# Expert loop of a two-layer block on one core: halves made by one engine less, rows gathered one expert earlier, and a branch hint on TensorE

## The chip, the cores and the metric

The kernel runs on one NeuronCore of a Trainium2 chip. The core has five engines that run side by side, each with an instruction stream of its own: TensorE (PE, matrix products; its weight loads are listed apart as PEld), VectorE (DVE), ScalarE (ACT), GpSimd (POOL) and SyncE (SP), which here issues DMAs. The metric is the device time of one execution in microseconds. It was 3232.24 us as the median of 3 runs (3224.29 to 3240.48).

## The reference

The reference is two transformer blocks on 512 tokens of width 1024, all in fp32. The first block has a hybrid mixer and then a mixture of experts, the second two attention layers with MLPs. The change touches the mixture of experts of the first block alone:

```python
def moe_ffn(h, router_w, router_bias, w_gate, w_up, w_down, ...):
    ...
    _, e_idx = lax.top_k(jnp.where(expert_mask, biased, -jnp.inf), TOP_K)      # 8 of 64 experts a token
    gate = jnp.take_along_axis(scores, e_idx, axis=1)
    gate = gate / jnp.sum(gate, axis=-1, keepdims=True) * ROUTED_SCALE
    ...
    def expert_block(args):                       # 128 rows of one expert
        xb, e = args
        return (jax.nn.silu(xb @ w_gate[e]) * (xb @ w_up[e])) @ w_down[e]
    ...
    routed = jax.ops.segment_sum(yb * row_gate[:, None], row_tok, num_segments=T + 1)[:T]
```

Each token goes to 8 of 64 experts, so an expert has 64 rows on average. The weights of an expert are 1024 x 512 (gate and up) and 256 x 1024 (down), 3 MB in fp32.

## The kernel before

A product in fp32 is made as three products: each operand is split into a high half (`hi`, rounded by ScalarE, L191) and the rest (`lo`, the difference, L192, by VectorE or POOL), and `mm3` (L220 to L222) multiplies hi by hi, hi by lo and lo by hi.

The weights of an expert come as three tiles of 1 MB (128 x 2048): two of gate and up, one of down. They land in a ring of 8 buffers (`raw`). SyncE issues them in order, in `fetch`; ahead of each it reads a word of the tile two issues back (L1144), so that no more than about two are under way. Each tile is split in two steps of 1024 columns, `halve` and `halve_to`. Of the down tile, the first step's `lo` is VectorE's and the second's POOL's; every other `lo` is VectorE's.

The rows of an expert are gathered from a table in memory by an indirect DMA of POOL (`gather`, L1213), up to 128 rows in a first block, and the results are added to an output table by another (`scatter`, L1218). The tile `cnt` holds the number of rows of each expert. `fewest` picks by comparisons on POOL a gather or scatter of 16, 32, ... 128 rows. `xg` is a list of four row buffers: two for the first blocks (`e % 2`), two for the others.

The loop over the experts is written out in Python, 64 experts and two more turns, under a manual schedule, so that every engine runs its part in the order of the code. In turn `e`:

- SyncE issues the down tile of expert `e + 1` and the gate and up tiles of `e + 2`;
- TensorE makes gate and up of expert `e` (24 products into `bank_g`), and all engines load the count of `e`;
- POOL gathers the first rows of expert `e + 2`; the halves of the down tile of `e` are made; the results of `e - 2` are copied out by ScalarE and scattered; the halves of the gate and up tiles of `e + 1` follow;
- then a branch of every engine on `n > 128` (L1377). The Then arm has a second block of 128 rows and, nested, a third and a fourth (`more_blocks`); the Else arm holds what most experts need: the transposes of the next expert's rows (`xT.turn`, L1255), the down product of `e - 1` (12 products), and the transposes of the activation (L1283).

On TensorE the Then arm, with its nested blocks, stands between the branch and the Else arm.

Of the kernel before, what the change touches and what calls it, by code (L numbers as in the profile page):

```python
# [10 lines left out]
F32 = mybir.dt.float32  # L11
# [9 lines left out]
D = 1024  # L21
NE = 64
T = 512
# [115 lines left out]
def body(tc, ins, out, stop=None, dump=None):  # L139
    nc = tc.nc  # L140
    top = ExitStack()
    V, S, G, PE = nc.vector, nc.scalar, nc.gpsimd, nc.tensor
# [10 lines left out]
    with top:  # L153
# [985 lines left out]
        def fetch(e, a):  # L1139

            if e < NE:
                ahead.append((e, a))
                if len(ahead) > 2 and ahead[-3] in raws:
                    nc.sync.value_load(raws[ahead[-3]][0:1, 0:1].bitcast(I32))  # L1144
                r = raws[e, a] = mp.tile([128, 2048], F32, tag="raw", bufs=8, name="raw")
                dma(r, ins["w_dn"][e] if a == 2 else ins["w_gu"][e, a])

        tt = mp.tile([128, 4, NE, 2], F32, name="tt")
        xg = xt
        with ExitStack() as st:  # L1150
            p = pool(st, "route")
            for e in range(2):
# [29 lines left out]
        with ExitStack() as st:  # L1182
# [54 lines left out]
                choose(0, 128)  # L1237

            def first_rows(e):
                fewest(e, gather, xg[e % 2])  # L1240

            def more_rows(e):
                with tc.If(rows(e) > 128):
                    gather(e, 1, xg[2 + e % 2])

            class Rows:

# [75 lines left out]
            st.enter_context(tc.manual_schedule())  # L1323
            for a in range(2):
                halve(0, a)
            for e in range(2):
                first_rows(e)
                more_rows(e)
            xT = Rows(xg[0], [psum("tr", 2) for _ in range(2)])
            xT.turn()  # L1330
            xT.halves()
# [4 lines left out]
            for t in (*pair, bank_t, bank_y):  # L1336
                V.memset(t, 0.0)
            y = None
            for e in range(NE + 2):
                if e == NE - 1:  # L1340

                    spare = [mp.tile([128, 2048], F32, tag="raw", bufs=8, name="raw") for _ in range(6)]
                    for j, src in enumerate((mod("m1", 5), ins["ln2_g"], ins["ln2_b"])):
                        load_row(spare[j // 2][:, j % 2 * D:(j % 2 + 1) * D], src)
                    for i in range(NT):
                        dma(spare[4 + i // 2][:, i % 2 * D:(i % 2 + 1) * D],
                            x1d[i * 128:(i + 1) * 128, :])
                if e < NE:
                    fetch(e + 1, 2)
                    fetch(e + 2, 0)  # L1350
                    fetch(e + 2, 1)
                    gate_up(gu[e], xT, bank_g)
                    n = nc.values_load(cnt[0:1, e:e + 1], min_val=0, max_val=T,
                                       engines=[E.PE, E.Activation, E.DVE, E.Pool])
                if e + 2 < NE:
                    first_rows(e + 2)
                if 0 < e <= NE:
                    act_halves(bank_t)
                if e < NE:
                    halve(e, 2, (V, G))  # L1360
                if e > 1:
                    y = rows_out(n=2)
                    down_out(pair, y)
# [5 lines left out]
                last = e == NE - 1  # L1369
                if not last:  # L1370
                    halve(e + 1, 0)
                    xT = Rows(xg[(e + 1) % 2], [psum("tr", 2) for _ in range(2)])
                    gu1 = [hl_tiles()]
                a = act(bank_g, e, 0)
                yx = rows_out("x")
                x = Rows(xg[2 + e % 2], (bank_x, bank_y))
                with tc.If(n > 128) as c:  # L1377

                    x.turn()
                    with tc.If(rows(e) > 256):  # L1380
# [17 lines left out]
                    with tc.If(n > 256):  # L1398
                        more_blocks(e, x, yx)
                        if not last:  # L1400

                            xT.halves()
                with c.Else():
                    if not last:
                        xT.turn()
                        xT.halves()
                    if e:
                        down(dn[e - 1], pair)
                    act_t(a, bank_t)
                    if not last:  # L1410
                        halve_to(gu1, e + 1, 1, 0)
# [527 lines left out]
```

## Time and profile before

| | us |
|---|---|
| median of 3 runs | 3232.24 |
| the profiled execution | 3234.01 |
| its span, first to last instruction | 3232.2 |
| expert stage, read as the window 960 to 1830 us | 870 |
| TensorE busy in that window | 744.23 |
| VectorE / ScalarE / POOL busy in that window | 642.38 / 573.62 / 390.15 |

The profiled execution is one run of the program; its span is 1.8 us shorter than its time. A busy time is the sum of the stretches in which an engine had an instruction at work. Idle time is given with its releaser, that is, with what the profile shows to have ended the wait.

### The profile page before, as it was taken

The numbers are of one execution on the slowest core, as the hardware profiler recorded it, in microseconds if no ns is written. First come the engines' busy times: TensorE is split into PE (matmuls) and PEld (weight loads), VectorE is DVE, ScalarE is ACT, GpSimd is POOL, SyncE is SP. The second block draws the span as 40 slices with busy tenths as digits, with TensorE's granted clock in tenths as the row PEclk, the third lists the DMA queues.
The fourth block names the chain that finished last, engine by engine and source line by source line (L and its number), as shares of the span: only waits on it lengthen the run. The fifth ranks groups of instructions, "written<-read, shape, count | busy, mean of one in ns | idle before, by whom it ended". The sixth has DMA issues, their size and how long they took to land. (4 is left out here: it accounts for less than half of the span.)

```text
span 3232.2 us, 42331 instructions
## 1 busy us (share of the span) xinstructions
PE 2914.3 (90%) x14268; PEld 2379.7 (74%) x14268; DVE 2118.9 (66%) x3558; ACT 1544.8 (48%) x2588; POOL 1115.8 (35%) x887
## 2 busy tenths in 40 slices
PE   7999999999778888988888579998999999889998
PEld 5887887877666766776667366676877788678887
DVE  8887876554748887885666469667554643774446
ACT  4443342555227676675665354545443434752222
POOL 3212211678334444453444321435453200320002
PEclk8999999999879999999999789998999999999999
DMA  6223314765348989897878522315443243332222
GB/s 238 74 73 118 135 68 161 243 236 204 138 155 290 315 266 299 272 322 243 288 243 273 154 89 78 110 52 199 172 161 136 72 144 111 106 109 88 91 91 72
DMA packets 142979, 540.44 MB, mean 167 GB/s; under 512 B 23809, under 2 KB 37121, under 8 KB 118017
## 3 DMA queue, kind: packets, MB, share of 16 engines
q1 hardware_dynamic: 106832, 422.21, 36.9%
q0 software_dynamic: 35760, 113.48, 12.5%
q8 instruction: 193, 3.16, 0.4%
q14 instruction: 194, 1.58, 0.2%
HBM read 509.43 MB, written 36.35 MB: 169 GB/s over the span
## 5 line engine op out<-in xcount | busy, mean ns | idle before, releaser
L192 DVE TENSOR_TENSOR lo<-raw,hi 128x1024 fp32r<-128x1024 f32 x615 | 873.8, 1439 | 453.0 <-ACT hi L191 447.0
L191 ACT CAST hi<-raw 128x1024 fp32r<-128x1024 f32 x697 | 716.3, 1053 | 477.9 <-PE mm L222 198.8
L221 PE MATMUL mm<-hlo,hi 128*128 128x512 f32 (+1 forms) x1448 | 539.2, 373 | 15.7 <-DVE hlo L962 15.7
L220 PE MATMUL mm<-hhi,hi 128*128 128x512 f32 (+1 forms) x1448 | 541.7, 376 | 5.1 <-ACT hhi L961 5.1
L222 PE MATMUL mm<-hhi,lo 128*128 128x512 f32 (+1 forms) x1448 | 538.1, 372 | 3.9 <-DVE lo L192 3.9
L221 PEld LDWEIGHTS mm<-hlo,hi 128*128 128x128 f32 x1448 | 281.7, 195 | 61.9 <-DVE hlo L962 16.8
L220 PEld LDWEIGHTS mm<-hhi,hi 128*128 128x128 f32 x1448 | 280.4, 194 | 55.4 <-ACT hhi L961 6.1
L222 PEld LDWEIGHTS mm<-hhi,lo 128*128 128x128 f32 x1448 | 281.3, 194 | 50.4 <-DVE lo L192 5.7
L355 POOL TENSOR_TENSOR ada_acc<-ada_acc,ada_w 128x512 f32<-128x512 f32 x168 | 248.5, 1480 | 138.7 <-ACT ada_acc L353 101.2
L192 POOL TENSOR_TENSOR lo<-raw,hi 128x1024 fp32r<-128x1024 f32 x82 | 208.1, 2542 | 153.2 <-ACT hi L191 82.9
L220 PE MATMUL mm<-hi,xh 128*128 128x512 f32 x584 | 235.3, 403 | 13.8 <-ACT xh L1262 5.5
L222 PE MATMUL mm<-hi,xl 128*128 128x512 f32 x584 | 231.0, 395 | 3.3 <-DVE xl L1263 3.3
L221 PE MATMUL mm<-lo,xh 128*128 128x512 f32 x584 | 229.2, 392 | 0.1
L220 PE MATMUL mm<-hi,fh 128*128 128x512 f32 x512 | 204.5, 399 | 11.2 <-ACT fh L191 5.6
L221 PE MATMUL mm<-lo,fh 128*128 128x512 f32 x512 | 203.5, 397 | 4.2 <-DVE lo L192 4.2
L222 PE MATMUL mm<-hi,fl 128*128 128x512 f32 x512 | 203.2, 397 | 1.1 <-DVE fl L192 1.1
L1218 POOL DMA_INDIRECT Rd<-ey,tt x73 | 142.6, 1953 | 157.4 <-POOLq L1398 78.0
L1213 POOL DMA_INDIRECT x<-h2d,tt x73 | 91.4, 1252 | 270.0 <-DVE lo L192 46.0
L1789 DVE TENSOR_TENSOR res<-mm,gr 128x512 f32<-128x512 f32 x64 | 44.2, 691 | 180.7 <-PE mm L222 180.7
L1255 PE MATMUL tr<-cst,x 128*128 128x128 f32 x512 | 81.4, 310 | 88.5 <-issue 76.6
L220 PE MATMUL mm<-hi,ah 128*128 128x512 f32 x338 | 152.9, 452 | 8.3 <-ACT ah L1287 4.3
L222 PE MATMUL mm<-hi,hlo 128*128 128x256 f32 (+1 forms) x512 | 160.3, 313 | 0.0
(794 smaller groups left out, 5975.0 us busy)
## 6 DMA issues: line engine op xcount, KB each, us to landing
raw<-in_w_gu SPq DMA_DIRECT2D x128, 1024.0 KB
raw<-in_w_dn SPq DMA_DIRECT2D x64, 1024.0 KB
raw<-in_mlp_w SPq DMA_DIRECT2D x128, 512.0 KB
ada_w<-in_ada_w POOLq DMA_DIRECT2D x96, 512.0 KB
raw<-in_w_in SPq DMA_DIRECT2D x88, 512.0 KB
ada_w<-in_w_ada POOLq DMA_DIRECT2D x64, 256.0 KB
raw<-in_b_w_in SPq DMA_DIRECT2D x24, 512.0 KB
w_ada<-in_w_ada SPq DMA_DIRECT2D x16, 512.0 KB
```

Source lines behind the costliest of these rows:

```text
L191: S.copy(hi, raw)
L192: eng.tensor_sub(lo, raw, hi.bitcast(F32))
L220: PE.matmul(ps, lh, rh, start=start, stop=False)
L221: PE.matmul(ps, lh, rl, start=False, stop=False)
L222: PE.matmul(ps, ll, rh, start=False, stop=stop)
L355: G.tensor_add(acc, acc, x)
L1213: G.indirect_dma_start(out=buf[0:n, :], out_offset=None, in_=h2d, in_offset=index(b, e, n), bounds_check=T - 1, oob_is_err=False)
L1218: G.indirect_dma_start(out=Rd, out_offset=index(b, e, n), in_=y[0:n, :], in_offset=None, compute_op=OP.add)
L1255: PE.transpose(self.banks[k // 4][:, k % 4 * 128:(k % 4 + 1) * 128], self.buf[:, k * 128:(k + 1) * 128], ident)
L1789: V.tensor_mul(t[:, c], ps[n], g[:, c])
```

## The change

Four things are changed, all in the expert stage. POOL no longer makes the second `lo` of the down tile: `halve(e, 2)` leaves both to VectorE. The first rows are gathered for expert `e + 3` instead of `e + 2`, into three buffers (`e % 3`), with a fifth buffer allocated for it and set to zero once. The weight ring has 7 buffers instead of 8. And TensorE gets a hint instruction for the branch of the next expert: the count of `e + 1` is loaded at the start of turn `e`, and at the head of both arms of expert `e` the comparison `counts[e + 1] > 128` goes into a register that the hint reads, for the branch with the label of expert `e + 1`; 0 in the register stands for a branch that is likely taken (to Else), 1 for one that is not.

```diff
--- before.py
+++ after.py
@@ -1142,11 +1142,13 @@
                 ahead.append((e, a))
                 if len(ahead) > 2 and ahead[-3] in raws:
                     nc.sync.value_load(raws[ahead[-3]][0:1, 0:1].bitcast(I32))
-                r = raws[e, a] = mp.tile([128, 2048], F32, tag="raw", bufs=8, name="raw")
+                r = raws[e, a] = mp.tile([128, 2048], F32, tag="raw", bufs=7, name="raw")
                 dma(r, ins["w_dn"][e] if a == 2 else ins["w_gu"][e, a])
 
         tt = mp.tile([128, 4, NE, 2], F32, name="tt")
-        xg = xt
+
+        xg = [*xt, mp.tile([128, D], F32, name="xg")]
+        G.memset(xg[4], 0.0)
         with ExitStack() as st:
             p = pool(st, "route")
             for e in range(2):
@@ -1237,11 +1239,11 @@
                 choose(0, 128)
 
             def first_rows(e):
-                fewest(e, gather, xg[e % 2])
+                fewest(e, gather, xg[e % 3])
 
             def more_rows(e):
                 with tc.If(rows(e) > 128):
-                    gather(e, 1, xg[2 + e % 2])
+                    gather(e, 1, xg[3 + e % 2])
 
             class Rows:
 
@@ -1323,9 +1325,10 @@
             st.enter_context(tc.manual_schedule())
             for a in range(2):
                 halve(0, a)
-            for e in range(2):
+            for e in range(3):
                 first_rows(e)
-                more_rows(e)
+                if e < 2:
+                    more_rows(e)
             xT = Rows(xg[0], [psum("tr", 2) for _ in range(2)])
             xT.turn()
             xT.halves()
@@ -1336,10 +1339,22 @@
             for t in (*pair, bank_t, bank_y):
                 V.memset(t, 0.0)
             y = None
+
+            def count(e):
+                return nc.values_load(cnt[0:1, e:e + 1], min_val=0, max_val=T,
+                                      engines=[E.PE, E.Activation, E.DVE, E.Pool])
+
+            def hint(e):
+
+                if e < NE:
+                    tc.mark_branch_hint_location(f"first{e}", counts[e] > 128, [E.PE])
+
+            counts = {0: count(0)}
+            hint(0)
             for e in range(NE + 2):
                 if e == NE - 1:
 
-                    spare = [mp.tile([128, 2048], F32, tag="raw", bufs=8, name="raw") for _ in range(6)]
+                    spare = [mp.tile([128, 2048], F32, tag="raw", bufs=7, name="raw") for _ in range(6)]
                     for j, src in enumerate((mod("m1", 5), ins["ln2_g"], ins["ln2_b"])):
                         load_row(spare[j // 2][:, j % 2 * D:(j % 2 + 1) * D], src)
                     for i in range(NT):
@@ -1349,15 +1364,16 @@
                     fetch(e + 1, 2)
                     fetch(e + 2, 0)
                     fetch(e + 2, 1)
+                    n = counts[e]
+                    if e + 1 < NE:
+                        counts[e + 1] = count(e + 1)
                     gate_up(gu[e], xT, bank_g)
-                    n = nc.values_load(cnt[0:1, e:e + 1], min_val=0, max_val=T,
-                                       engines=[E.PE, E.Activation, E.DVE, E.Pool])
-                if e + 2 < NE:
-                    first_rows(e + 2)
+                if e + 3 < NE:
+                    first_rows(e + 3)
                 if 0 < e <= NE:
                     act_halves(bank_t)
                 if e < NE:
-                    halve(e, 2, (V, G))
+                    halve(e, 2)
                 if e > 1:
                     y = rows_out(n=2)
                     down_out(pair, y)
@@ -1369,12 +1385,13 @@
                 last = e == NE - 1
                 if not last:
                     halve(e + 1, 0)
-                    xT = Rows(xg[(e + 1) % 2], [psum("tr", 2) for _ in range(2)])
+                    xT = Rows(xg[(e + 1) % 3], [psum("tr", 2) for _ in range(2)])
                     gu1 = [hl_tiles()]
                 a = act(bank_g, e, 0)
                 yx = rows_out("x")
-                x = Rows(xg[2 + e % 2], (bank_x, bank_y))
-                with tc.If(n > 128) as c:
+                x = Rows(xg[3 + e % 2], (bank_x, bank_y))
+                with tc.If(n > 128, label=f"first{e}") as c:
+                    hint(e + 1)
 
                     x.turn()
                     with tc.If(rows(e) > 256):
@@ -1401,6 +1418,7 @@
 
                             xT.halves()
                 with c.Else():
+                    hint(e + 1)
                     if not last:
                         xT.turn()
                         xT.halves()
```

On TensorE, the Else arm of the first expert and the start of the next expert's gate and up stood so before (`tr` is the bank of the transposed rows, `cst` the unit matrix, `ea` the activation; a row of matmuls stands for its weight loads too):

```order
L1255 MATMUL tr<-cst,x_7333 128x128 x8
L1283 MATMUL sm<-cst,ea_8677 128x128 x2
L1377 UNCONDITIONAL_BRANCH
L1243 UNCONDITIONAL_BRANCH
L220 MATMUL mm<-hi,xh 128x512
L221 MATMUL mm<-lo,xh 128x512
```

On TensorE the same place stands so in the changed kernel:

```order
L1350 REGISTER_ALU
L1953 BRANCH_PREFETCH_HINT
L1257 MATMUL tr<-cst,x_7333 128x128 x8
L1285 MATMUL sm<-cst,ea_8679 128x128 x2
L1393 UNCONDITIONAL_BRANCH
L1344 TENSOR_LOAD cnt
L1344 ISA x2
L1245 UNCONDITIONAL_BRANCH
L220 MATMUL mm<-hi,xh 128x512
```

The arm now begins with the comparison and the hint, and the load of a count stands ahead of the products. Before, that load stood behind all 24 products, next to the branch.

On VectorE, the work of the second expert up to its activation stood so before (`al` is the low half of the activation, `L1353` the load of the count):

```order
L1353 TENSOR_LOAD cnt
L1288 SCALAR_TENSOR_TENSOR al<-sm,ah 128x256
L192 TENSOR_TENSOR lo<-raw,hi 128x1024
L1232 UNCONDITIONAL_BRANCH
L192 TENSOR_TENSOR lo<-raw,hi 128x1024 x2
L1276 SCALAR_TENSOR_TENSOR ea_8677<-ea_8677,mm 128x256
L1277 SCALAR_TENSOR_TENSOR ea_8677<-ea_8677,tt,mm 128x256
```

On VectorE the same place stands so in the changed kernel:

```order
L1344 TENSOR_LOAD cnt
L1290 SCALAR_TENSOR_TENSOR al<-sm,ah 128x256
L192 TENSOR_TENSOR lo<-raw,hi 128x1024 x2
L1234 UNCONDITIONAL_BRANCH
L192 TENSOR_TENSOR lo<-raw,hi 128x1024 x2
L1278 SCALAR_TENSOR_TENSOR ea_8679<-ea_8679,mm 128x256
L1279 SCALAR_TENSOR_TENSOR ea_8679<-ea_8679,tt,mm 128x256
```

Behind `al` there are now two subtractions of the down tile in place of one; the two after them are those of the next expert's first tile.

## Rows read from the trace of the kernel before

**Rows 1.** The page, part 1: busy time in us, share of the span and number of instructions of each engine.

```profile
PE 2914.3 (90%) x14268; PEld 2379.7 (74%) x14268; DVE 2118.9 (66%) x3558; ACT 1544.8 (48%) x2588; POOL 1115.8 (35%) x887
```

**Rows 2.** Busy time by window of the expert stage (start and end in us), with the granted clock of TensorE (1.00 is full), the share of the DMA engines and GB/s. The first window is the stage, the other two are stretches in it.

```profile
core 0: us, PE busy (x) PEld busy (x) DVE busy (x) ACT busy (x) POOL busy (x), PEclk, DMA share, GB/s
960.00:1830.00 870.00, 744.23 (x3350) 593.73 (x3350) 642.38 (x692) 573.62 (x825) 390.15 (x207) 0.94 0.84 274
1000.00:1100.00 100.00, 87.91 (x400) 69.90 (x399) 88.42 (x88) 74.83 (x105) 51.26 (x26) 0.95 0.95 318
1240.00:1460.00 220.00, 191.20 (x874) 153.14 (x874) 182.20 (x185) 156.51 (x222) 111.81 (x60) 0.95 0.90 300
```

**Rows 3.** Who waited for whom in the window 960 to 1830 us: us in total, times, longest us. PEld is the weight load of TensorE, PE its matmul; "issue" is time in which the engine waited for nothing that the profile shows.

```profile
PEld tr L1255 <- issue: 99.4, 29, 5.7
...
PE tr L1255 <- issue: 76.6, 21, 5.3
...
PE tr L1255 <- DMA x<-h2d,tt: 10.7, 4, 5.0
...
PE sm L1283 <- DVE ea L1277: 8.1, 16, 1.4
```

**Rows 4.** The instructions of line 1377, the branch on the number of rows: times in ns, least/median/most, first and last start in us. PEldq and ACTq are the sequencers of TensorE and ScalarE.

```profile
L1377 PEldq COMPARE_BRANCH  x64: 70/429/7357, 968.3 to 1817.7; - x64
L1377 ACTq COMPARE_BRANCH  x64: 40/45/50, 973.3 to 1821.0; - x64
```

**Rows 5.** The page, part 3, the queue of the instruction packets of 16 KB: packets, MB, time as a share of 16 engines' span.

```profile
q8 instruction: 193, 3.16, 0.4%
```

**Rows 6.** TensorE in order of time from 1410 to 1428 us, two experts without a second block: start us, us, engine, line, operation, tile, count, and in brackets the idle time before it and what ended it.

```profile
1412.47 1.04 PE L1255 MATMUL tr<-cst,x 128*128 128x128 f32 x8
...
1414.05 0.39 PE L220 MATMUL mm<-hi,ah 128*128 128x512 f32 x1
...
1421.59 0.39 PE L222 MATMUL mm<-hi,xl 128*128 128x512 f32 x1
1424.91 1.94 PE L1255 MATMUL tr<-cst,x 128*128 128x128 f32 x8 [2.94 <-issue]
...
1427.93 0.49 PE L220 MATMUL mm<-hi,ah 128*128 128x512 f32 x1
```

**Rows 7.** Busy time by window as in rows 2, ahead of the stall of rows 6 and after it.

```profile
1411.00:1421.00 10.00, 10.00 (x51) 8.30 (x50) 9.50 (x11) 9.18 (x14) 7.23 (x4) 1.00 0.89 312
1424.70:1428.10 3.40, 3.19 (x12) 2.93 (x13) 2.65 (x5) 1.75 (x3) 1.84 (x1) 0.50 1.06 375
```

**Rows 8.** Groups of instructions of the window 960 to 1830 us, by line and shape: count, busy us, mean ns of one, idle us of the engine before them and what ended it.

```profile
L192 DVE TENSOR_TENSOR lo<-raw,hi 128x1024 fp32r<-128x1024 f32 x321 | 472.0, 1500 | 135.2 <-ACT hi L191 133.7 <-ACT ey L1300 1.0
...
L192 POOL TENSOR_TENSOR lo<-raw,hi 128x1024 fp32r<-128x1024 f32 x64 | 160.8, 2512 | 72.2 <-ACT hi L191 68.4 <-issue 2.4 <-DVE lo L192 0.3
...
L1263 DVE TENSOR_TENSOR xl<-tr,xh 128x512 fp32r<-128x512 f32 x130 | 85.1, 686 | 51.6 <-ACT xh L1262 47.3 <-issue 3.3
...
L1277 DVE SCALAR_TENSOR_TENSOR ea<-ea,tt,mm 128x256 f32<-128x256 f32 x73 | 35.1, 481 | 2.6
L1288 DVE SCALAR_TENSOR_TENSOR al<-sm,ah 128x256 fp32r<-128x256 f32 x73 | 30.4, 417 | 3.0 <-ACT ah L1287 3.0
L1276 DVE SCALAR_TENSOR_TENSOR ea<-ea,mm 128x256 f32<-128x256 f32 x73 | 30.0, 412 | 44.8 <-ACT ea L1275 41.8 <-ACTq L1377 3.0
```

**Rows 9.** VectorE in order of time, columns as in rows 6.

```profile
1398.81 3.48 DVE L192 TENSOR_TENSOR lo<-raw,hi 128x1024 fp32r<-128x1024 f32 x3
1402.21 0.41 DVE L1276 SCALAR_TENSOR_TENSOR ea<-ea,mm 128x256 f32<-128x256 f32 x1
...
1403.05 1.28 DVE L1263 TENSOR_TENSOR xl<-tr,xh 128x512 fp32r<-128x512 f32 x2
...
1415.79 3.53 DVE L192 TENSOR_TENSOR lo<-raw,hi 128x1024 fp32r<-128x1024 f32 x2
...
1419.58 5.72 DVE L192 TENSOR_TENSOR lo<-raw,hi 128x1024 fp32r<-128x1024 f32 x3
```

**Rows 10.** POOL in order of time, columns as in rows 6.

```profile
1414.69 2.40 POOL L192 TENSOR_TENSOR lo<-raw,hi 128x1024 fp32r<-128x1024 f32 x1
...
1421.65 2.57 POOL L192 TENSOR_TENSOR lo<-raw,hi 128x1024 fp32r<-128x1024 f32 x1
```

**Rows 11.** SyncE's own waits in the window 960 to 1830 us, columns as in rows 3. L1144 reads a word of an earlier weight tile, L151 is the issue of a DMA.

```profile
SPq L1144 <- DMA raw<-in_w_gu: 355.9, 110, 5.8
SPq L1144 <- DMA raw<-in_w_dn: 193.4, 52, 6.0
SPq L151 <- DVE al L1288: 107.2, 21, 21.3
SPq L151 <- POOL lo L192: 78.7, 19, 9.4
```

**Rows 12.** SyncE's DMA issues in order of time, columns as in rows 6.

```profile
1012.75 0.33 SPq L151 DMA_DIRECT2D raw<-in_w_dn  x1
...
1103.47 0.33 SPq L151 DMA_DIRECT2D raw<-in_w_dn  x1
```

**Rows 13.** The transposes of the rows of a second, third or fourth block, which are those that write the bank `mm` (four a block): times in ns, first and last start in us.

```profile
L1255 PE MATMUL mm<-cst,x x36: 270/272/273, 1120.3 to 1769.3; 128*128 128x128 f32 x36
```

## The prediction

> **What bounds the kernel now.** I read the page first, then the windows, the waits, the branch's own line, and last the timeline around one stall. The page's first part [rows 1] has TensorE busy for 90% of the span, so only its idle time and its slow time can be won. All the lines of the change lie in the expert stage; its window, 960 to 1830 us [rows 2], is 870 us long with TensorE busy for 744.2, hence idle for 126. The waits of that window [rows 3] say for what: 76.6 us in 21 pieces stand before the transposes of L1255 and are put down to "issue", which means that nothing in the profile was being waited for; 10.7 us in 4 pieces wait at the same line for gathered rows, and 8.1 us in 16 for the activation that VectorE makes.
>
> What the 76.6 us are is read from the branch `n > 128` of L1377 [rows 4]. On ScalarE that branch takes 45 ns. On TensorE's sequencer the median is 0.43 us and the longest 7.36 us. One stall is in [rows 6]: the last matmul of an expert starts at 1421.59 us, and the first transpose of the Else arm at 1424.91, 2.94 us after the engine ran dry. This looks like code that was not loaded. The queue of instruction packets [rows 5] carries 193 packets with 3.16 MB, 16.4 KB each. The built order has 23,342 matmuls on TensorE; with a weight load each and some 1,700 other instructions that is 48,400, or 250 to a packet. Between the branch and its Else arm stand 160 matmuls, 320 instructions or 1.28 packets. If only the packet in use and the next one are held, an Else arm lies beyond both in 28% of the cases: 15 or 16 of the some 56 experts that have no second block. That is near enough to the 21 pieces.
>
> The Trainium skill (Runtime: NRT & Kernel Launch, section Instruction fetch mechanics) says just this: code comes in 16 KiB blocks of 256 instructions, two are held, and a taken branch that leaves both waits for a fetch. The packets' size agrees. The same section gives TensorE room for 2,048 instructions; with that, a jump over 330 would never miss, and the stalls in the trace speak against it.
>
> **The change part by part.** *Hint.* Both arms of an expert now begin with two sequencer instructions, a comparison into a register and the hint, and the load of the next count moves ahead of gate and up. Four such steps of at most 0.3 us an expert run in a sequencer that is ahead of its engine: the branches of 0.43 us cost TensorE no idle time at all, so I cost them at nothing (without that cover 64 x 0.3 = 19 us). The order now has the hint 46 matmuls, hence about one expert's work, ahead of the branch that it speaks of. From [rows 6], transposes at 1412.47 to the engine running dry at 1421.97, that is 9.5 us; the slowest branch needed 7.36. So a fetch that starts at the hint is in time, and up to 76.6 us go.
>
> *The clock after a stall.* While a stall lasts and some microseconds after, the granted clock is 0.50, the lower level of 1.2 GHz; in the busy stretch ahead it was 1.00 [rows 7]. Eight transposes and three matmuls took 1414.05 - 1412.47 = 1.58 us at the upper level and 1427.93 - 1424.91 = 3.02 us after the stall [rows 6]: 1.44 us more. I take that for 15 long stalls of the 21: 22 us.
>
> *Rows three experts ahead.* The gather gets one expert more, about 9.5 us, and the longest of the four waits was 5.0 us. I take 9 of the 10.7 us. It is issued by POOL behind the same things as before; the third buffer was last read one expert earlier, so no wait is added. One more gather and one memset stand ahead of the loop, where TensorE is still at the shared expert: nothing.
>
> *No halves on POOL.* POOL loses 64 subtractions, 160.8 us [rows 8], and VectorE gets them. Alone it makes three in 3.48 us, 1.16 each; beside POOL's own, three take 5.72 and two 3.53 [rows 9, 10]. Its 321 subtractions stand at 472.0 us, where 321 x 1.16 would be 372; after, 385 x 1.16 = 447. So VectorE gains 25 us in sum though it does more. In one expert it then has 6 x 1.16 + 1.28 (both xl) + 0.41 + 0.48 + 0.41 = 9.54 us [rows 8, 9] beside TensorE's 9.50. That is a near tie, and the first wait to show once the stalls are gone: TensorE at L1283 for VectorE's activation, 8.1 us now. Bounds: all 8.1 us go, or another 0.7 us comes in each of 55 experts (the order of 1.16 less the slack that the interference leaves), +38. I take 0.
>
> *Seven weight buffers for eight.* SP waits 549 us for the landing of earlier weights and, at the `dma` of L151, for buffers whose last reader is late, 107.2 and 78.7 us among them [rows 11]. One buffer less makes the second kind longer. Behind the waiting `dma` on SP stand only later weights. What it costs depends on the pace of the weights: the down weights of two experts eight apart were issued at 1012.75 and 1103.47 us [rows 12], 24 transfers at 3.78 us, while SP mostly waited for landings and the DMA share was 0.95 [rows 2]. Three make 11.3 us an expert. TensorE and VectorE would like 9.9 (an estimate from the 9.5 above and some 0.4 of remaining waits). The second blocks, nine by [rows 13], each add about as much again and let the weights catch up, but none comes before 1120 us. The first 13 experts therefore use up what lies ready. In sum the weights need 185 x 3.78 = 699 us, and TensorE 870 - 76.6 - 22 - 9 = 762: not the bound overall, but in stretches of a dozen plain experts each lacks up to 1.4 us, 17 us less the two experts of stock. For two or three such stretches I add 15 us (0 to 45).
>
> **Sum.** -76.6 - 22 - 9 + 15, and +13 for stalls that stay (about a sixth, where the hint comes too late): -80. The profiled execution took 3234.0 us (span 3232.2 and 1.8 around it), so 3154; the median shown is 1.8 below it, which makes 3152 us.
>
> **The rivals.**
> *The hint does nothing.* In the trace each packet came in the program's order; nothing shows a fetch out of order. If the fetcher only goes on in sequence, the stalls stay, and -9 for the gathers, 0 for the halves and a few us for the lost buffer remain: 3225 us. The Trainium skill, in the section named above, calls the prefetch purely sequential; by that rule the hint is empty, and no run here shows a hint yet.
>
> *The weights set the pace.* The stage moves 238 MB (870 us at 274 GB/s). In 1240 to 1460 us the DMA ran at 300 GB/s with a share of 0.90 [rows 2]; at that rate 238 MB take 794 us, and the last expert's work of about 30 us comes after the last landing: 824 us, -46, 3186 us. For it: the share of 0.95. Against it: 318 GB/s was reached for 100 us on end.
>
> *Slower: the hint takes the place of the next block.* If two packets are all that is held, fetching the hinted one may throw out the sequential one that is needed first. That happens where a packet ends between hint and branch, 95 instructions or 0.38 packets, so in 24 of 63 experts. Each would then wait as one of the stalls now, 76.6 / 21 = 3.6 and 1.44 for the clock: 24 x 5.1 = +121, less the 80 gained, +41: 3273 us. It decides the sign from about 16 such waits on. Against it: the old packet is not needed any more when the arm begins, which leaves its place for one of the two.
>
> **How the numbers follow.** The forecast has 0.52 (its own range 3125 to 3180), the weights' pace 0.20, the empty hint 0.18, the lost block 0.10. The low end is everything at its best, -76.6 - 22 - 10.7 - 8 = -117, hence 3112; the high end, 3232, takes in the empty hint and leaves the slower case out. A measurement of this kernel tells about 0.5%, 16 us, from no change. Faster by more: 0.52 + 0.20 and 0.01 of the empty hint, 0.73. Within: nearly all of the empty hint, 0.16. Slower: 0.11.
>
> **What would show it.** Right: the branch's longest time on TensorE falls from 7.36 to under 1 us, "issue" before the transposes nearly vanishes, the stage's granted clock rises from 0.94 towards 0.98, POOL's subtractions are gone and those of VectorE take 1.2 us each, and ScalarE's first halves begin to wait for `raw` now and then. The expert stage is then about 790 us long. Wrong: branches that still take 6 us (the hint is empty), new "issue" waits at L220 to L222 (a block was thrown out), waits of ScalarE for `raw` over 45 us in sum (the weights' pace), or L1283 waiting over 40 us for VectorE (it is the bound).

## The result, and the profile after

The changed kernel takes 3152.39 us (median of 4 runs, 3149.36 to 3163.50), the kernel before 3235.05 us in the same comparison (4 runs, 3224.29 to 3240.48): a ratio of 0.9763, 95% interval 0.9734 to 0.9792. The forecast was 3152.

The profiled execution has a span of 3147.6 us. Its page, parts 1 and 3, answers to [rows 1, 5]:

```profile
PE 2882.1 (92%) x14268; PEld 2353.3 (75%) x14268; DVE 2112.0 (67%) x3622; ACT 1542.0 (49%) x2588; POOL 941.9 (30%) x824
...
q8 instruction: 192, 3.15, 0.4%
```

The branch's own line [rows 4], least/median/most in ns (line numbers of the changed kernel are higher: its L1393 is L1377 of before, L1257 is L1255, L1285 is L1283):

```profile
L1393 PEldq COMPARE_BRANCH  x64: 70/1570/6795, 965.0 to 1737.2; - x64
```

Here is the surprise. From first to last branch the stage is 1737.2 - 965.0 = 772.2 us, where it was 1817.7 - 968.3 = 849.4, but the branch did not get faster: its longest time is 6.80 us (7.36 before), and its median rose from 0.43 to 1.57 us. Still the waits have shrunk (expert stage, 957 to 1750 us, TensorE and ScalarE, against [rows 3]):

```profile
PE tr L1257 <- issue: 26.5, 12, 3.4
ACT hi L191 <- DMA raw<-in_w_gu: 14.9, 13, 2.0
...
ACT hi L191 <- DMA raw<-in_w_dn: 8.2, 8, 2.4
PE sm L1285 <- DVE ea L1279: 7.1, 12, 1.4
PE tr L1257 <- DMA x<-h2d,tt: 6.8, 4, 2.3
```

SyncE waits more for landings and less for buffers than in [rows 11]:

```profile
SPq L1144 <- DMA raw<-in_w_gu: 392.0, 116, 6.2
SPq L1144 <- DMA raw<-in_w_dn: 205.4, 59, 6.7
SPq L151 <- DVE al L1290: 54.1, 14, 18.2
```

The windows from the first to the last branch, of the kernel before:

```profile
968.30:1817.70 849.40, 731.29 (x3304) 584.11 (x3303) 632.06 (x678) 560.87 (x806) 381.55 (x203) 0.94 0.84 276
```

and of the changed kernel (columns as in [rows 2]):

```profile
965.00:1737.20 772.20, 704.13 (x3303) 564.49 (x3302) 613.07 (x742) 558.63 (x807) 208.81 (x139) 0.98 0.93 305
```

For the same matmuls TensorE is busy 27.2 us less, at a granted clock of 0.98 for 0.94, and idle for 68.1 us instead of 118.1. Of these 50.0 us, "issue" before the transposes gives 50.1 (76.6 to 26.5). The subtractions of VectorE [rows 8] are more but shorter, and those of POOL are gone; the whole stage again, 957 to 1750 us:

```profile
L192 DVE TENSOR_TENSOR lo<-raw,hi 128x1024 fp32r<-128x1024 f32 x385 | 454.4, 1220 | 93.2 <-ACT hi L191 89.5 <-ACT ey L1302 1.7 <-issue 0.3
```

That the branch waits for code is in the DMA records of the two traces, which give a start and a landing for each instruction packet of q8 (but not which code it holds). Before, 27 of the 64 branches took over 1 us, and each of the 27 ended 1.3 to 1.6 us after a packet had landed; of the other branches the median ended 4.6 us after one. In the changed kernel it is 36 branches, and each ended 1.3 to 1.7 us after a landing. For 22 of the 27 and 28 of the 36, the transfer of that packet had not even begun when the branch started; between the first and the last branch no two packets started less than 2.7 us apart.

How can a branch that is as slow as before cost less? Two stalls side by side tell it. In the one of [rows 6], the line of the count's load and that of the branch, cut to this one expert, read:

```profile
L1353 PEldq TENSOR_LOAD <-cnt x1: 301/301/301, 1419.4 to 1419.4; - x1
```

```profile
L1377 PEldq COMPARE_BRANCH  x1: 4642/4642/4642, 1420.1 to 1420.1; - x1
```

VectorE's last two subtractions ended at 1415.79 + 3.53 = 1419.32 us [rows 9], with one of POOL's beside them from 1414.69 to 1417.09 [rows 10]. TensorE's sequencer, which had to see the last `lo` before it could queue the products that read it, began the load at 1419.4 and the branch 0.7 us later. That is no accident of one expert: at 59 of the 64 branches this load begins within 0.15 us of the end of one of VectorE's subtractions, and after the change the branch itself does at 62 of 64. TensorE ran dry at 1421.59 + 0.39 = 1421.98: 1.9 us of queued work hid the first part of the branch. The packet that it waited for started at 1422.41 and landed at 1423.39, and the branch ended at 1424.75. A stall of the changed kernel has this branch:

```profile
L1393 PEldq COMPARE_BRANCH  x1: 6795/6795/6795, 1412.4 to 1412.4; - x1
```

VectorE ahead of it (in order of time, columns as in [rows 6]):

```profile
1409.74 1.23 DVE L192 TENSOR_TENSOR lo<-raw,hi 128x1024 fp32r<-128x1024 f32 x1
1411.15 1.23 DVE L192 TENSOR_TENSOR lo<-raw,hi 128x1024 fp32r<-128x1024 f32 x1 [0.19 <-ACT hi L191]
```

and TensorE behind it:

```profile
1416.02 0.39 PE L222 MATMUL mm<-hi,xl 128*128 128x512 f32 x1
1419.60 1.94 PE L1257 MATMUL tr<-cst,x 128*128 128x128 f32 x8 [3.19 <-issue]
```

The last `lo` ends at 1412.38, the branch begins at 1412.4 with no load in between, and TensorE has work until 1416.41. Now 4.0 us of the branch are hidden. (Its packet started at 1416.44, landed at 1417.76, and the branch ended at 1419.24.) It took 2.2 us longer than the other and cost 0.25 us more (3.19 for 2.94). The theory after the result was therefore: the code still comes as late as before, the hint does little, and the gain comes from two things that let the sequencer reach the branch sooner, the early load of the count and the subtractions that POOL no longer makes beside VectorE's. The rival was the prediction's: the hint fetches the code.

### The profile page after: what moved, and what is told of

Same layout as the page of the kernel before. It is cut to its first block, busy times and chain, and to the rows that moved or that the text cites. A ratio compares the mean times of both kernels' runs of the same rounds, so it can differ in the third digit from the quotient of the medians.

```text
span 3147.6 us, 42222 instructions
## 1 busy us (share of the span) xinstructions
PE 2882.1 (92%) x14268; PEld 2353.3 (75%) x14268; DVE 2112.0 (67%) x3622; ACT 1542.0 (49%) x2588; POOL 941.9 (30%) x824
## 3 DMA queue, kind: packets, MB, share of 16 engines
q0 software_dynamic: 35760, 113.48, 12.9%
## 5 line engine op out<-in xcount | busy, mean ns | idle before, releaser
L192 DVE TENSOR_TENSOR lo<-raw,hi 128x1024 fp32r<-128x1024 f32 x679 | 861.9, 1295 | 403.4 <-ACT hi L191 399.4
L1220 POOL DMA_INDIRECT Rd<-ey,tt x73 | 124.2, 1701 | 257.1 <-POOLq L1415 63.1
L220 PE MATMUL mm<-hi,hhi 128*128 128x256 f32 (+1 forms) x512 | 159.0, 311 | 0.0
L221 PE MATMUL mm<-lo,hhi 128*128 128x256 f32 (+1 forms) x512 | 158.7, 310 | 0.0
L353 ACT ACTIVATE ada_w<-ada_w,cs 128x512 f32<-128x512 f32 x168 | 110.5, 713 | 97.8 <-DMA ada_w<-in_ada_w 96.5
```

The lines of the kernel that those rows point to most:

```text
L192: eng.tensor_sub(lo, raw, hi.bitcast(F32))
L220: PE.matmul(ps, lh, rh, start=start, stop=False)
L221: PE.matmul(ps, lh, rl, start=False, stop=False)
L353: S.activation(x if kk else acc, x, AF.Copy, scale=cs[:, kk:kk + 1])
L1220: G.indirect_dma_start(out=Rd, out_offset=index(b, e, n), in_=y[0:n, :], in_offset=None, compute_op=OP.add)
```

## The experiments

All medians are of 5 or 6 runs (split: 9, changed: 4; before: 11 in the row shown); the kernel before had 3233 to 3235 us in these comparisons, and each ratio is to the kernel before in its own comparison. "Stage" is from the start of the first to that of the last branch, from the branch's line as shown above; "issue" is TensorE's wait of that name before the transposes of the rows, us and times.

| kernel | median, us | ratio (95%) | stage, us | issue |
|---|---|---|---|---|
| before | 3233.69 | | 849.4 | 76.6, 21 |
| before + early count | 3202.98 | 0.9911 (0.9890 to 0.9932) | 819.4 | 59.6, 19 |
| before + VectorE's halves | 3188.67 | 0.9868 (0.9843 to 0.9894) | 805.1 | 56.4, 18 |
| before + both | 3157.91 | 0.9761 (0.9734 to 0.9789) | 773.6 | 40.7, 17 |
| before + early count + hint | 3190.76 | 0.9866 (0.9843 to 0.9890) | 794.7 | 10.1, 4 |
| changed, no hint | 3159.26 | 0.9769 (0.9746 to 0.9791) | 766.3 | 32.6, 12 |
| changed | 3152.39 | 0.9763 (0.9734 to 0.9792) | 772.2 | 26.5, 12 |
| changed, hint turned round | 3172.37 | 0.9812 (0.9781 to 0.9842) | 785.1 | 48.5, 21 |
| changed, hint later | 3151.16 | 0.9734 (0.9710 to 0.9758) | 770.1 | 19.1, 7 |
| changed, hint between | 3156.17 | 0.9754 (0.9729 to 0.9779) | 762.4 | 13.5, 7 |
| changed + load by the branch | 3174.47 | 0.9823 (0.9796 to 0.9849) | 791.9 | 49.7, 16 |
| changed + POOL's subtraction | 3181.91 | 0.9841 (0.9814 to 0.9869) | 790.0 | 15.4, 8 |
| changed, no fourth block | 3173.57 | 0.9807 (0.9780 to 0.9834) | 770.9 | 32.8, 11 |
| changed, split jump | 3212.78 | 0.9937 (0.9914 to 0.9961) | 820.2 | 0 |

The rest of the program, the median less the stage, is not quite the same in all of them: 2384 us for the first four, 2380 for the changed kernel, 2392 to 2396 for five others, 2403 without the fourth block. In a stretch of the second block TensorE's granted clock was 0.96 in the changed kernel and 0.94 in the last of these. What sets that is open, so a difference of medians of 10 us alone says little; the stage is read beside it. Stage and "issue" are of one profiled execution each, and have no interval.

One thing is not held still in all of these. Which branches wait depends on where they stand in their packets (see the shorter jump below). By the traces TensorE ran 29,103 instructions in the kernel before and in the three with the early count, VectorE's halves and both, and 29,239 in the changed kernel, with the hint turned round and with POOL's subtraction; taking the hint out or adding it changes that by 128, the load by the branch by 192, and other experts' branches wait then. What such a shift alone is worth was not run, so the rows that involve one are weaker evidence than the others.

### The hint taken out

```diff
             def hint(e):
-                if e < NE:
-                    tc.mark_branch_hint_location(f"first{e}", counts[e] > 128, [E.PE])
+                return
```

> The changed kernel without its hint instructions; the early load of the counts, the gathers three experts ahead, the 7 buffers and VectorE's halves stay. If the hint brings the code of the Else arm in ahead of the branch (the theory of the prediction), the stalls come back: 'issue' before the transposes about 77 us instead of 27, the time 3152 + 50 to 75 = about 3215. If the hint is empty and the gain comes from the count being loaded earlier, so that TensorE's sequencer reaches the branch sooner and hides part of each fetch, nothing changes: 3152 within 8, 'issue' about 27 us, longest branch 6.8 us.

3159.26 us; the intervals of the two ratios nearly coincide. The branch stayed about as it was, and the stage is 766.3 us, 6 shorter than with the hint, so the 7 us of the median lie outside it:

```profile
L1392 PEldq COMPARE_BRANCH  x64: 70/1766/7736, 972.0 to 1738.3; - x64
```

"Issue" is 32.6 us, 6 more than with the hint. The stalls that the prediction ascribed to the hint do not come back. With hint or without, the packet that a waiting branch needs starts late, at a median of 1.5 and 1.8 us behind the start of the branch.

### The early count alone

```diff
-                    gate_up(gu[e], xT, bank_g)
-                    n = nc.values_load(cnt[0:1, e:e + 1], ...)
+                    n = counts[e]
+                    if e + 1 < NE:
+                        counts[e + 1] = count(e + 1)
+                    gate_up(gu[e], xT, bank_g)
```

> The kernel before with one edit: the count of the next expert is loaded at the start of a turn, ahead of gate and up, instead of behind them next to the branch. If the hint is what helps, this stays at 3235 within 10. If the earlier load lets the sequencer start the fetch sooner, by some 1 to 2 us in each of 21 stalls and with the slow clock behind each, 3235 - 30 to 60 = about 3190, and the 'issue' before the transposes falls from 77 to 30 to 50 us.

3202.98 us, 31 less: the second theory, at the low end of its 30 to 60. "Issue" fell less than the 30 to 50 us expected:

```profile
PE tr L1255 <- issue: 59.6, 19, 4.9
```

The packet that a waiting branch needs starts at a median of 2.5 us behind the start of the branch, 2.8 before: when the branch came sooner, its packet did too.

### VectorE's halves alone

```diff
-                    halve(e, 2, (V, G))
+                    halve(e, 2)
```

> The kernel before with one edit: VectorE makes both halves of the down tile, POOL none. By the prediction this is worth nothing: 3235 within 8, VectorE's subtractions 447 us in the stage in place of 472. If VectorE were near its limit it would be up to 38 us slower; if POOL's subtractions held up the products by way of VectorE, up to 8 us (what waits there now) faster, or more where POOL's late halves feed the down product.

3188.67 us: the largest single part, 45 us, from an edit that was costed at nothing. The subtractions go from 1.50 us [rows 8] to 1.23 (1.16 had been worked out), and their sum stays about what it was; the second line is "issue" before the transposes:

```profile
L192 DVE TENSOR_TENSOR lo<-raw,hi 128x1024 fp32r<-128x1024 f32 x388 | 461.1, 1226 | 94.2 <-ACT hi L191 86.3 <-issue 6.2
PE tr L1255 <- issue: 56.4, 18, 5.8
```

### Both

> The kernel before with two edits, the early load of the counts and both halves of the down tile by VectorE; gathers two ahead, 8 buffers, no hint. If these two make the gain and the gathers and the seventh buffer are worth nothing, 3159 within 8, as the changed kernel without the hint. If both act by letting TensorE's sequencer arrive at the branch sooner, the matmuls queued ahead of it at a missing branch last 4.0 us at most where they were 2.3 before and 3.0 with one of the edits. If the gathers matter, 3170 or more.

3157.91 us, 75 less than before, and 31 + 45 = 76: the two add up. With this the gathers, the seventh buffer and the hint together are left with 5.5 us, inside what the measurement can tell. "Issue" before the transposes:

```profile
PE tr L1255 <- issue: 40.7, 17, 3.8
```

Counted over the 64 branches, when the sequencer comes to the branch (or to the load just ahead of it) a median of 12 products are still to start on TensorE before the change and with the early count 14.5, with VectorE's halves 15, with both 16.

### The early count and the hint, without the rest

```diff
+                hint(e + 1)      # at the head of both arms
```

> The kernel before with the early count and the hints in both arms; POOL keeps its halves, the gathers stay two ahead, 8 buffers stay. If the hint helps, most of the gain is here: about 3165, with 'issue' under 30 us. If the hint is empty, the same as the kernel with the early count alone, within 6 us.

3190.76 us, 12 less than with the early count alone: more than the 6 of an empty hint, and 26 short of the 3165 of one that works. Here "issue" nearly vanishes, so this hint is not empty. The packet that a waiting branch needs now starts at a median of 0.4 us behind the start of the branch, 2.5 with the early count alone, and 25 branches over 1 us remain for 27, most of them shorter. Yet of the 49.5 us less of "issue" the stage keeps 24.7 (794.7 for 819.4), and 12 of these are lost again outside the stage, for which no run shows a reason. The waits of TensorE show one place where the first part goes:

```profile
PE tr L1255 <- DMA x<-h2d,tt: 27.2, 15, 3.8
PE tr L1255 <- issue: 10.1, 4, 4.7
```

With the early count alone the first of these was 8.1 us in 7 pieces: when the code is there, the rows gathered two experts ahead are not always. With the gathers three ahead, in the changed kernel, that wait is 6.8 us; the hint with these gathers and with POOL's halves was not run.

### The hint turned round

```diff
-                    tc.mark_branch_hint_location(f"first{e}", counts[e] > 128, [E.PE])
+                    tc.mark_branch_hint_location(f"first{e}", counts[e] <= 128, [E.PE])
```

> The changed kernel with the hint's comparison turned round, so that the hint names the other arm for every expert; the code is of the same length. If the hint fetches what it names, this fetches the wrong arm for 56 of 63 experts: slower than the kernel without the hint (3159), by 10 us or more, with longer branches. If the hint is empty, 3152 to 3160, and the 'issue' before the transposes 25 to 33 us as with the right hint and without any.

3172.37 us. "Issue" is 48.5 us, against 32.6 with no hint and 26.5 with the right one. The code is of the same length as with the right one and only the hint's sense differs, so the chip acts on the hint:

```profile
PE tr L1257 <- issue: 48.5, 21, 4.1
```

The stage is 12.9 us longer than with the right hint and the median 20, though the intervals of the two ratios still overlap a little. 194 packets came instead of 192, but as many came with the right hint at the later place below, so their number does not tell it.

### The hint at two later places

```diff
+                    hint(e)      # later: ahead of the products
                     gate_up(gu[e], xT, bank_g)
...
-                    hint(e + 1)      # at the head of both arms
```

> The changed kernel with the hint moved from the head of the arms to just ahead of the 24 products of gate and up, some 50 instructions and 5.5 us ahead of its branch. If the hint brings in the packet it names, and from the head of the arm it comes too early (the packets still needed in sequence are fetched ahead of it or thrown out), here it should shorten most stalls: idle time before the transposes from 37 us to under 20, 3152 - 15 to 35 = about 3130. If a hint is worth nothing wherever it stands, 3152 to 3160, as with none.

> The changed kernel with the hint behind the down products of an arm, ahead of the transposes of the activation, which lies between the two places. If hints work and the place decides, between the two: about 3140. If a hint is worth nothing, 3152 to 3160.

3151.16 us later, 3156.17 us between the two places, behind the down products. Neither met 3130 or 3140, although "issue" fell to 19.1 and 13.5 us; these are as the changed kernel within the intervals. The packet of a waiting branch starts at a median of 1.0 us behind the start of the branch in both.

### One load put back beside the branch

```diff
                     gate_up(gu[e], xT, bank_g)
+                    nc.values_load(cnt[0:1, e:e + 1], ..., engines=[E.PE])
```

> The changed kernel with one more load of the count on TensorE's sequencer alone, behind the 24 products, where the load stood before; its value is not used. If the early load helped because TensorE's sequencer comes to the branch 0.7 us sooner, that goes again: the matmuls queued at a missing branch last 3.3 us at most in place of 4.0, and the time rises by 15 to 30. If it helped by the loads of ScalarE, VectorE and POOL, which stay early here, 3152 within 8.

3174.47 us, 22 more, by 0.7 us in a sequencer and nothing on any engine (and by three more instructions a turn in TensorE's code). The work queued at a branch of over 3 us is 3.3 to 3.5 us at most, where it is 4.0 in many in the changed kernel. The wait is back as well:

```profile
PE tr L1257 <- issue: 49.7, 16, 5.4
```

With the early count, which shifts no code, that points to the place of TensorE's load; the loads of the other engines stayed early here.

### A subtraction given to POOL again, of nothing

```diff
+        idle = mp.tile([128, 1024], F32, name="idle")
...
                     halve(e, 2)
+                    G.tensor_sub(idle, idle, idle)
```

> The changed kernel with one subtraction of 128 x 1024 on POOL added in every turn, on a tile of its own that nothing else reads (zeros), so that VectorE still makes all halves. If what helped was that POOL's subtraction no longer slows VectorE's beside it (VectorE's last half is late, TensorE's sequencer waits for it and comes late to the branch), much of the gain goes again: 3152 + 20 to 45, VectorE's subtractions 1.35 us or more in place of 1.22 and the matmuls queued at a missing branch 3.0 us in place of 4.0. If what helped was the down tile's second half being made earlier, or POOL being free for gathers and scatters, 3152 within 8, or up to 10 more by the gathers.

3181.91 us, 30 more; in the stage alone 17.8. Nothing reads what POOL makes, and yet VectorE's subtractions got slower (lines one and two; the third is "issue" before the transposes):

```profile
L192 DVE TENSOR_TENSOR lo<-raw,hi 128x1024 fp32r<-128x1024 f32 x388 | 532.7, 1418 | 67.4 <-ACT hi L191 63.6 <-DMA Rd<-ey,tt 3.1
L1379 POOL TENSOR_TENSOR idle<-idle 128x1024 f32<-128x1024 f32 x64 | 126.1, 1971 | 9.0 <-POOLq L1346 4.6 <-DMA x<-h2d,tt 2.7
PE tr L1259 <- issue: 15.4, 8, 3.5
```

64 of POOL's at 1.97 us are 126 us; VectorE's 388 took 71.6 us longer in sum than in the kernel with VectorE's halves alone. A median of 12 products is left when the sequencer comes to the branch, as before the change and not 15. So the interference may account for a good part of the 45 us (17.8 in the stage, 30 in the median); as "issue" fell instead of rising, the loss is not of the form that I expected, and how the interference costs its time stays open. TensorE's busy time rose by 11 us at the same clock, which is most of the 17.8, and I have not found why.

### A shorter jump

Without the code of the fourth block (its gather and its `more_blocks`), as the expectation says:

> The changed kernel without the code of the fourth block of rows, which no expert of these inputs needs (none has over 384 rows). The jump from the branch to the Else arm is 114 matmuls, hence some 230 instructions, in place of 160 and some 330, and so less than one packet of 256. If the stalls are code that is not loaded, most of them go: 'issue' before the transposes under 8 us in place of 26.5, the longest branch under 4 us, the time 3152 - 20 to 45 (with the slow clock behind the long stalls) = about 3120. If the weights' transfers now set the pace, or the stalls are something else, 3152 within 8.

The stage is 770.9 us, as with the fourth block (772.2), and the longest branch is still 7.4 us:

```profile
L1387 PEldq COMPARE_BRANCH  x64: 70/374/7401, 976.4 to 1747.3; - x64
```

The median branch is fast again: 18 branches take over 1 us, half as many as with the fourth block, but each of the 18 takes 3.6 us or more, though the jump is shorter than a packet by the estimate above. "Issue" is 32.8 us, far from the 8 expected. The median time is 21 us longer, all of it outside the stage. My picture of two packets held, of which a jump under one packet cannot get out, fails here. Each of the 18 branches ends 1.3 to 1.4 us after a packet has landed, and that packet's transfer started 1.2 to 5.0 us after the branch had: the next packet was not there yet. The 18 are every third expert from 3 to 57 (counted from 0), save 51, which has a second block. So where a branch stands in its packet decides whether it waits, more than the length of the jump.

### One jump made two

```diff
-                    with tc.If(n > 256):          # inside the Then arm
-                        more_blocks(e, x, yx)
...
+                with tc.If(n > 256):              # behind the Else arm
+                    more_blocks(e, x, yx)
...
```

> The changed kernel with the third and fourth block moved out of the Then arm, under a branch of their own behind the Else arm; nothing is left out. One jump of some 330 instructions becomes two of some 140 and 190, each under a packet. If only the length of a jump matters, the stalls nearly go: 3152 - 15 to 40. If the packets, fetched one after the other at about 6 us each, are themselves too slow for 1.7 of them an expert of 10 us, the waits move to the second jump and the time stays within 10 of 3152 or rises by the extra branch on four engines.

3212.78 us, 60 more than the changed kernel. No stall is left at the transposes (the longest branch is 3.8 us, 4.2 at the second jump), but a skipped arm has semaphores to set on every engine, and now each plain expert skips one more. ScalarE waits for VectorE's at the new branch (L1425):

```profile
ACT ah L1289 <- DVEq L1425: 30.0, 30, 1.7
```

and TensorE for ScalarE in its turn:

```profile
PE mm L220 <- ACT ah L1289: 33.4, 37, 2.6
PE mm L220 <- ACT hi L191: 17.8, 19, 1.3
```

Of the engines POOL takes longest over it: 2.0 us of its sequencer for each of 63 skipped arms, on top of what it did for the first branch. ScalarE's waits for the landing of scatters, which POOL issues, are 49.5 us, in the changed kernel 8.9:

```profile
L1425 POOLq INC_SWDGE_SEM  x63: 966/2037/2717, 962.8 to 1788.8; - x63
ACT ey L1302 <- DMA Rd<-ey,tt: 49.5, 21, 5.5
```

How the 60 us divide between these chains was not separated.

## Why the time was right and the reasons were not

**What bounds the kernel: right.** The 76.6 us were TensorE without code behind a branch, and that is what fell; the landings of the packets show it. The count of 15 or 16 experts, worked out from two packets held, was low: 27 branches took over 1 us, and the shorter jump shows that one packet away is not always near enough.

**The hint (-76.6, of which +13 were to stay): the step that failed.** "So a fetch that starts at the hint is in time" does not hold: branches of up to 6.8 us remain. The stalls fell by 50 us, but taking the hint out gives back 6 of these and 7 us of the median, and the intervals overlap; with the hint, the packet that a waiting branch needs still starts 1.5 us behind the branch's start in the median. The signs named for it failed with it: the branch is not under 1 us, and "issue" has not nearly vanished. The rival with an empty hint was closer in its cause for this kernel; its 3225 us was wrong, because it left the early load and the halves at nothing, as the forecast did. Its ground, that each packet came in the program's order, can't be read from the trace, which does not tell what a packet holds.

**The early load, "I cost them at nothing": 31 us.** The step counted only what four more sequencer instructions cost. It did not ask what was taken away from beside the branch: 0.7 us between the last product and a branch that then waits for code. The median branch cost TensorE no idle time, as the text said; the long ones are hidden only as far as the queue reaches, 1.9 us in the stall before and 4.0 in the one after.

**No halves on POOL, "I take 0": 45 us, beyond the bound of -8.** The sizes were nearly right: 1.22 us a subtraction for 1.16, a sum of 454 us for 385 where 447 was worked out. But the step compared sums of an expert, 9.54 against 9.50 us, and took the waits at L1283 for the price. What mattered was when the last `lo` is ready. TensorE's engine did not wait for it in the rows; its sequencer did, and came late to the branch (12 products left in the queue before, 15 with VectorE's halves). That this is the whole of the 45 us is not shown: POOL's idle subtraction brought the 12 back and cost 30, without the "issue".

**The clock, -22: right in size, 27 measured** as TensorE's busy time. Between the first and the last branch the clock was granted at 0.50 in 20 stretches of 106 us in sum before, in 9 of 38 us after, so each hidden microsecond counted for more than one. One reading was wrong: while the stall of [rows 6] lasted, the clock stood at 1.00 until 1424.4 us; it was 0.50 behind it, from 1424.9 to 1427.8, where the sum charged it.

**The gathers (-9) and seven buffers (+15): near nothing together.** The wait for gathered rows fell by 3.9 us, to 6.8. ScalarE's waits for weights are 23.1 us in sum, under the 45 named, and the changed kernel without the hint stands 1.4 us from the one with both main edits.

**The sum** was met by luck: the early load and the halves, both put at nothing, made 75 us of the 82.7, and the hint, the gathers and the buffers together 5.5. By the rows of the trace -63.6 for the stalls became -50.1, -22 for the clock -27.2, and -9 for the gathers -3.9; other waits of TensorE rose by 4.0, which makes the 77.2 us of the stage, and about 5 us more came from outside it, for which the sum had no term. No +15 for the buffers shows. The low end of the range was added up wrongly: -117 from 3232 is 3115 us, not 3112. The other signs held: granted clock 0.98, POOL's subtractions gone, VectorE's 1.22 us.

The Trainium skill (Runtime: NRT & Kernel Launch, section Instruction fetch mechanics) calls the prefetch purely sequential. By that rule a hint would be empty, and here the runs differ: added to the early count it takes "issue" from 59.6 to 10.1 us, and turned round in the changed kernel from 26.5 to 48.5. So a hint moves the fetch, whether out of the sequence or only sooner the traces do not tell. It is nearly worthless in this kernel all the same: 3 to 12 us of time in four kernels. Why 13 to 19 us less of "issue" with the two later hints bring no measurable time was not settled.

## What to carry to other kernels

An engine that shows no wait for another can still be made late by it through its sequencer: ahead of a branch, ask when the last operand arrives and what stands between it and the branch, since queued work is what hid the fetch here. Take loads of registers away from a branch, and take a second engine's subtractions away from beside the engine that makes the last operand. And when one change has several parts, time them apart, even if the sum agrees with the forecast: here the hint, with the largest price in the sum, was worth about 7 us in the changed kernel, and two parts at nothing were worth 75.

## What the runs showed of the hardware

- POOL's subtraction of two tensors slows VectorE's beside it, also when they share no data: 1.42 us with it, 1.23 without. The Trainium skill (GPSIMD Engine Reference, section 1. Specifications) names this contention for VectorE's instructions with two inputs in SBUF, and the trace agrees with these numbers.
- 0.7 us of TensorE's sequencer ahead of the branch cost 22 us in the median, 64 x 0.34 us, with a shift of the code by 192 instructions in it; taking the loads of all engines away from there in the kernel before, with no such shift, gave 31 us.
- Each of TensorE's branches of over 1 us ended 1.3 to 1.7 us after an instruction packet had landed (27 before, 36 in the changed kernel), and in these two kernels no two packets started less than 2.7 us apart in the stage.
- A taken branch over less than one packet of code (an estimate: some 230 instructions of about 250) can wait 7.4 us, as long as one over 1.3 packets; with the shorter jump every third expert's waited.
- A branch hint on TensorE takes 35 ns and is acted on; the wrong one cost 20 us against the right one (13 in the stage) and about 13 against none (19 in the stage).
- A skipped arm took 2.0 us of POOL's sequencer (INC_SWDGE_SEM, 63 times) in the kernel with the split jump, against 17 to 51 ns of the other engines'.
